# Second block's expert stage: routing's rest behind the second unit and its loads behind the first fetched rows; first block: rows split by VectorE instead of GpSimd

## The chip, the core and the metric

The kernel runs on one core of a Trainium2 chip. Its time is the device time of one execution in microseconds (us). Engines: TensorE (PE) multiplies matrices, VectorE (DVE) and ScalarE (ACT) work on tiles, GpSimd (POOL) does small things and issues indirect DMAs, SyncE (SP) issues the weight loads. Each engine runs its own instructions in a fixed order and waits on semaphores.

## What is computed

A transformer of 512 tokens by 1024 features, all in float32: a first block (mixer, cross attention, a mixture of experts), then a second block of two layers (token mixer, a mixture of experts). The change touches the three expert stages. Each picks for a token one of 4 groups and in it 2 of 8 experts; in the reference:

```
p_top, g_idx = lax.top_k(softmax(h @ w_rg + b_rg), 1)
e_top, e_local = lax.top_k(e_logits_of_group(g_idx), 2)
weights = p_top * softmax(e_top)
out[t] += weights * ((silu(x[t] @ w_gate[e]) * (x[t] @ w_up[e])) @ w_down[e])
```

An expert's hidden width is 512 in the first block (its three matrices are 2 MB each) and 256 in the second (1 MB each). In the second block, the token's row after the mixer is normalised, used by the experts, and also scaled by alpha, gain and bias for the residual sum.

## The kernel before

The expert stage (function moe, called by moe1 and moe2) works in units. A unit is up to 128 slots, shared by 2 or 3 experts (32 to 96 slots each); the second block has 14 units. Experts are ranked by how many tokens chose them, and the table of units says which rank gets how many slots. Experts 0 and 1 (second block) or 0 to 3 (first block) have fixed places, so their weights are loaded before routing is known; every other expert number is read by SP from a table (tab) that the routing computes.

Ahead of the stage, proj_cols multiplies by the output projection. After each of the four token tiles m, half(m, 1) makes the router's logits, the row factors (trs, with a power on GpSimd), chooses groups and experts (choose, a chain of small VectorE operations that ends in ohb), and writes the rows: in the second block to DRAM (zd), in the first by split_rows into a high part and a low part (xhi, xlo), which PE later multiplies with one-hot matrices.

route() then ranks experts and gives each token its slots. In the second block begin() turns the slots of unit 0 into token numbers and issues the indirect DMA that fetches its 128 rows (load_rows, tile xg, 0.5 MB). The rest of the routing is the function rest(): gate weights with two exponentials on ScalarE, slots of the overflow, a transpose on PE (L1156), two broadcasts on PE (L1164) into rows 2 and 3 of R["rows"], from which slot_weights makes the factor ws of each unit, and the expert table of the overflow.

The loop over units (L1552 and on) does for unit u: load gate and up weights and run unit_up (PE L1266, then hid, the transposes hT of L1272), fetch(u + 3), turn_rows of unit u + 1 (PE L1384, ScalarE L1386), and unit_down of unit u - 1 (yp L1291, yh and yl scaled by ws, then comb L1300/L1301, added to x). Order matters in two ways: the program order and priorities decide each engine's instruction order, and SP's queue is served in order, so a load that waits holds all loads behind it. Tiles for weights come from 5 + 6 buffers; a load waits until PE has freed its buffer.

In unit 0 of the second block a piece is put behind the last fetch's instruction (got["last"]): rest() and, for each tile, rows(m), two VectorE operations over 1024 columns that make the residual rows (L1684, L1685). In the first block rest() stands in the same place without rows(m).

Of the kernel before, what the change touches and what calls it, by code (L numbers as in the profile page):

```python
# [8 lines left out]
F32 = mybir.dt.float32  # L9
# [4 lines left out]
AF = mybir.ActivationFunctionType  # L14
OP = mybir.AluOpType
# [59 lines left out]
class Net:  # L75
# [910 lines left out]
    def split_rows(self, z, scale, m, hi, lo):  # L986

        h3, l3 = [t[m // 2][:, m % 2 * 1024:m % 2 * 1024 + 1024].rearrange("t (k p) -> t k p", k=8) for t in (hi, lo)]
        n = 1024 if scale is None else 512
        for a in range(0, 1024, n):  # L990
            src, p = z[:, a:a + n], slice(a // 8, (a + n) // 8)
            if scale is not None:
                t = self.k2("zs")
                self.nc.scalar.activation(t, src, AF.Copy, scale=scale)
                src = t
            src = src.rearrange("t (p k) -> t k p", k=8)
            self.nc.scalar.activation(h3[:, :, p], src, AF.Copy)
            last = self.nc.gpsimd.tensor_tensor(l3[:, :, p], src, h3[:, :, p].bitcast(F32), op=OP.subtract)
        return last

    def chooser(self):

# [237 lines left out]
    def load(self, W, e, k0, ahead, t=None, cols=slice(None)):  # L1240

        k, n = W.shape[1] // 128, W.shape[2]
        kn = 2048 // n
        if t is None:
            t = self.wtile(kn, n, ahead)
        src = W[e:e + 1] if isinstance(e, int) else W[bass.ds(e, 1)]
        self.nc.sync.dma_start(t[:, :, cols], src.rearrange("o (p k) n -> p (o k) n", k=k)[:, k0:k0 + kn, cols])
        return t

    def unit_up(self, xe, at, cols, wt, F, picking=None):  # L1250
# [138 lines left out]
    def moe(self, x, y, Wo, measure, norm, router, Wg, Wu, Wd, F, block, alpha=None, rows=None, prep=None, finish=None):  # L1389
# [11 lines left out]
        dram = block == 2  # L1401
        if dram:
            zd = self.keep.tile([512, 1024], F32, name="zd", tag="zd", bufs=2)
# [6 lines left out]
        else:  # L1410
            hi, lo = [[self.b8(n, F32R) for _ in range(2)] for n in ("xhi", "xlo")]
        lps = self.paux("lps")
        L, choose, choice = self.chooser()
        stats, split = {}, {}
        copy = nc.vector.tensor_copy if ws is None else (lambda o, i: nc.scalar.activation(o, i, AF.Copy))

        self.loaded, self.early = {}, {}

        def loads():
            for k0 in range(0, 8, 2048 // F):  # L1420
                for key, W in (("g", Wg), ("u", Wu)):
                    for e in (0, 1):
                        self.early[key, e, k0] = self.load(W, e, k0, True)
# [18 lines left out]
        def half(m, c):  # L1442
            with self.tc.high_priority():
                self.logits(x[m], m, c, wr, lps, copy)
                stats[m] = measure(m, c)
            if c:
                shift, rs = stats[m]
                off = rb
                with self.tc.high_priority():
                    if shift is not None:  # L1450
                        off = L[:, m, 4:40]
                        nc.vector.scalar_tensor_tensor(off, ws, shift, rb, op0=OP.mult, op1=OP.add)
                    for i in (m, 4 + m):
                        nc.vector.scalar_tensor_tensor(L[:, m, 4:40], lps[:, i * 36:i * 36 + 36], rs, off, op0=OP.mult, op1=OP.add)
                        off = L[:, m, 4:40]
                    choose(m)
                    if static == 4:
                        static_slots(m)
                left = norm(m, *stats[m])
                if dram:  # L1460
                    nc.scalar.dma_start(zd[m * 128:(m + 1) * 128, :], x[m])
                else:
                    split[m] = self.split_rows(x[m], left, m, hi, lo)

        self.proj_cols(y, Wo, self.add_to(x, alpha), lambda m: half(m, 0), lambda m: half(m, 1), loads)
        for e in (0, 1) if block == 1 else (0,):
# [8 lines left out]
        got = {}  # L1475
# [15 lines left out]
            with self.tc.high_priority():  # L1491
                one_hot(S0, 256, got[0], range(3, 4))
        def begin(S2):
            got["first"], _ = self.load_rows(zd, self.first_tokens(S2))

        R, rest = self.route(L, choice, self.tables[block], begin if dram else None)
        S2 = R["S2"]
# [14 lines left out]
        def expert(at):  # L1512
            return nc.values_load(R["tab"][0:1, at], engines=[mybir.EngineType.SP], min_val=0, max_val=31)
# [5 lines left out]
        def own_rows(at):  # L1519
            if dram:  # L1520
                return DTs.pop(at if isinstance(at, float) else "more"), self.slot_weights(R["rows"], at)
            return self.slot_rows(R, at)

        def before_down(es, at, ahead=True):
            return self.unit_weights("d", Wd, es, ahead), *own_rows(at)

        def down(hT, cols, es, at, ahead=True, finish=None, pre=None):
            wt, DT, ws = pre or before_down(es, at, ahead)
            self.unit_down(hT, cols, wt, F, DT, ws, x, finish)
# [14 lines left out]
        def fetch(u):  # L1544
            if u < len(units):
                DTs[128.0 * u], rowsof[u], _, got["last"] = self.fetch(zd, R["rows"], 128.0 * u)
# [17 lines left out]
        for u, unit in enumerate(units):  # L1564
            es = [(r, r if r < static else expert(slice(r, r + 1))) for r, _ in unit]
            cols, a0 = [], 0
            step = 32 if len({w for _, w in unit}) > 1 else unit[0][1]
            for i, (_, w) in enumerate(unit):
                cols += [(a0 + a, step, i) for a in range(0, w, step)]
                a0 += w  # L1570
            last = u == len(units) - 1
            if last:
                pre = before_down(*late[0][2:])
                down(*late.pop(), pre=pre)
                after = own_rows(128.0 * u)
            now = up(*((xe[u // 2][:, u % 2], 0) if dram else (xe[u // 2], u % 2 * 128)), cols, es), cols, es, 128.0 * u
            if last:
                pre = self.unit_weights("d", Wd, es, True, 2), *after
            if u == 0:
                if dram:  # L1580
                    with self.tc.issue_after(got["last"].ins):
                        rest()
                        for m in range(4):
                            rows(m)
                else:
                    with self.tc.issue_after(got["last"].ins):
                        rest()
            if u == 8 and prep is not None:
                prep()
            if dram:  # L1590
                fetch(u + 3)
                turn(u + 1)
            elif u % 2 and u + 1 < len(units):
                xe[u // 2 + 1] = pick(u + 1)
            while len(late) > (u in LAG[block]):
                down(*late.pop(0))
            late.append(now)
# [4 lines left out]
        n = nc.values_load(R["tab"][0:1, 64:65], min_val=0, max_val=32)  # L1602
        with self.tc.For_i(0, n) as iv:
            es, cols = [("further", expert(bass.ds(iv + 32, 1)))], [(0, 128, 0)]
# [683 lines left out]
```

## Time and profile before

| | us |
|---|---|
| median of 3 runs (2622.02 to 2631.01) | 2626.03 |
| profiled execution | 2632.68 |
| its span | 2630.8 |
| PE busy (92% of the span) | 2419.8 |
| VectorE busy (53%) | 1400.1 |
| ScalarE busy (35%) | 925.2 |
| GpSimd busy (10%) | 272.0 |

The stages follow one another: the first block's expert stage lies between about 430 and 1000 us of the span, those of the second block between about 1490 and 1800 and between 2300 and 2610. All times of rows are microseconds from the span's start. A wait is idle time of an engine, put down to what ended it. The clock column is the granted TensorE clock as a share of full speed: 1.00 is 2.4 GHz, 0.50 is 1.2 GHz.

### The profile page before, as it was taken

How to read it: one execution, taken by the hardware profiler on the slowest of the kernel's cores; microseconds unless marked ns; L12 is line 12 of the kernel's file. 1: busy time of each engine (PE TensorE's matmuls, PEld its weight loads, DVE VectorE, ACT ScalarE, POOL GpSimd, SP SyncE). 2: the span in 40 equal slices, each digit the busy share in tenths (PEclk: the TensorE clock that was granted, in tenths of full speed). 3: DMA queues.
4: the chain of work that ended last, by engine and by line, in shares of the span. 5: the costliest groups of instructions: out<-in, count | busy, mean ns of one | idle time of the engine just before them, and what ended most of it. 6: DMA issues, size and time to landing. Idle time of an engine off the chain costs nothing. (4 is left out here: it accounts for less than half of the span.)

```text
span 2630.8 us, 37791 instructions
## 1 busy us (share of the span) xinstructions
PE 2419.8 (92%) x14261; PEld 1579.4 (60%) x14261; DVE 1400.1 (53%) x3094; ACT 925.2 (35%) x1825; POOL 272.0 (10%) x444
## 2 busy tenths in 40 slices
PE   7898998899889998999999789998899999969995
PEld 6787887533334346677788644545577778735552
DVE  5568535432223236865645555446865644665455
ACT  6545533201111013655444132224554543322222
POOL 1143021000010001000020100104100010000001
PEclk9999999999999988999999889999999999979998
DMA  5214322779999976122223479994312223378993
GB/s 179 80 65 142 118 80 98 298 316 403 408 404 406 406 297 183 40 57 72 65 96 122 176 310 374 413 408 122 102 49 64 72 89 120 136 283 345 419 419 142
DMA packets 153047, 551.20 MB, mean 210 GB/s; under 512 B 20539, under 2 KB 48473, under 8 KB 105243
## 3 DMA queue, kind: packets, MB, share of 16 engines
q1 hardware_dynamic: 144458, 523.68, 52.1%
q0 software_dynamic: 6960, 20.33, 2.2%
q10 hardware_dynamic: 1440, 4.72, 0.5%
q8 instruction: 114, 1.87, 0.3%
q14 instruction: 75, 0.61, 0.1%
HBM read 538.19 MB, written 10.49 MB: 209 GB/s over the span
## 5 line engine op out<-in xcount | busy, mean ns | idle before, releaser
L248 DVE TENSOR_TENSOR wlo<-raw,whi 128x512 fp32r<-128x512 f32 (+2 forms) x368 | 258.4, 707 | 306.5 <-ACT whi L247 269.7
L247 ACT ACTIVATE whi<-raw 128x512 fp32r<-128x512 f32 (+2 forms) x368 | 215.8, 590 | 418.7 <-PE pacc L268 299.6
L267 PE MATMUL pacc<-hbh,whi 128*128 128x512 f32 (+1 forms) x768 | 309.2, 403 | 0.2 <-ACT whi L247 0.2
L269 PE MATMUL pacc<-hbh,wlo 128*128 128x512 f32 (+1 forms) x768 | 304.7, 397 | 1.1 <-DVE wlo L248 1.1
L268 PE MATMUL pacc<-hbl,whi 128*128 128x512 f32 (+1 forms) x768 | 304.0, 396 | 0.0
L1266 PE MATMUL gp<-we,xe 128*32 128x256 f32 (+3 forms) x2264 | 262.6, 433 | 5.7 <-DMA we<-in_w_gate_dram 5.0
L1303 DVE TENSOR_TENSOR x<-comb,x 128x512 f32<-128x512 f32 x304 | 191.7, 685 | 36.3 <-PE comb L1301 34.4
L1266 PE MATMUL gp<-wx,xe 128*32 128x256 f32 (+3 forms) x1608 | 201.9, 420 | 0.0
L1266 PEld LDWEIGHTS gp<-we,xe 128*32 128x32 f32 (+1 forms) x2264 | 113.2, 118 | 119.8 <-issue 62.8
L1268 ACT ACTIVATE hid<-gp 128x256 f32<-128x256 f32 (+1 forms) x41 | 18.5, 452 | 445.1 <-PE gp L1266 445.1
L1291 PE MATMUL yp<-we,hidT 128*32 128x512 f32 (+1 forms) x824 | 173.1, 605 | 1.1 <-ACT hidT L1274 0.7
L267 PEld LDWEIGHTS pacc<-hbh,whi 128*128 128x128 f32 (+1 forms) x768 | 144.3, 188 | 41.8 <-issue 8.5
L269 PEld LDWEIGHTS pacc<-hbh,wlo 128*128 128x128 f32 (+1 forms) x768 | 144.4, 188 | 36.1 <-issue 2.9
L268 PEld LDWEIGHTS pacc<-hbl,whi 128*128 128x128 f32 (+1 forms) x768 | 144.7, 188 | 31.3 <-issue 2.0
L1300 PE MATMUL comb<-yh,DT 128*128 128x512 f32 x328 | 135.8, 436 | 6.5 <-ACT yh L1293 6.2
L1294 DVE SCALAR_TENSOR_TENSOR yl<-yp,ws,yh 128x512 fp32r<-128x512 f32 x82 | 60.5, 749 | 144.3 <-ACT yh L1293 131.7
L1269 DVE TENSOR_TENSOR hid<-up,hid 128x512 f32<-128x512 f32 x13 | 9.0, 692 | 218.5 <-PE up L1266 218.5
L1291 PE MATMUL yp<-wx,hidT 128*32 128x512 f32 (+1 forms) x568 | 123.3, 602 | 1.6 <-ACT hidT L1274 1.0
L1301 PE MATMUL comb<-yl,DT 128*128 128x512 f32 x328 | 122.4, 400 | 1.9 <-DVE yl L1294 1.9
L1266 PEld LDWEIGHTS gp<-wx,xe 128*32 128x32 f32 (+1 forms) x1608 | 83.8, 113 | 55.8 <-issue 32.6
L1300 PEld LDWEIGHTS comb<-yh,DT 128*128 128x128 f32 x328 | 60.4, 188 | 86.9 <-ACT yh L1293 39.2
L1266 PE MATMUL up<-we,xe 128*32 128x512 f32 (+1 forms) x336 | 93.5, 645 | 13.5 <-DMA we<-in_w_up_dram 13.5
(704 smaller groups left out, 4693.2 us busy)
## 6 DMA issues: line engine op xcount, KB each, us to landing
raw<-in_w_in_dram SPq DMA_DIRECT2D x44, 1024.0 KB, 5.0
we<-in_w_down_dram SPq DMA_DIRECT2D x43, 1024.0 KB
we<-in_w_gate_dram SPq DMA_DIRECT2D x39, 1024.0 KB
we<-in_w_exp_up_dram SPq DMA_DIRECT2D x34, 1024.0 KB, 21.0
wx<-in_w_exp_gate_dram SPq DMA_DIRECT2D x34, 1024.0 KB, 20.9
we<-in_w_up_dram SPq DMA_DIRECT2D x33, 1024.0 KB, 4.9
wx<-in_w_exp_down_dram SPq DMA_DIRECT2D x32, 1024.0 KB, 10.2
wx<-in_w_up_dram SPq DMA_DIRECT2D x31, 1024.0 KB, 11.7
```

Source lines behind the costliest of these rows:

```text
L247: nc.scalar.activation(hi[:, :ncols], src, AF.Copy)
L248: nc.vector.tensor_tensor(lo[:, :ncols], src, hi[:, :ncols].bitcast(F32), op=OP.subtract)
L267: nc.tensor.matmul(o, hi[:, a], h.hi(k)[:, :ntok], start=k == 0, stop=False)
L268: nc.tensor.matmul(o, hi[:, a], h.lo(k)[:, :ntok], start=False, stop=False)
L269: nc.tensor.matmul(o, lo[:, a], h.hi(k)[:, :ntok], start=False, stop=k == kt - 1)
L1266: nc.tensor.matmul(ps[s:s + w, :], xe[:, k, at + s:at + s + w], wt[key, i, k], start=k == 0, stop=k == 7)
L1268: nc.scalar.activation(h, gp, AF.Silu)
L1291: nc.tensor.matmul(yp[a:a + w, :], hT[:, k * 128 + a:k * 128 + a + w], d, start=k == 0, stop=k == nf - 1)
L1294: nc.vector.scalar_tensor_tensor(yl[c], yp, ws, yh[c].bitcast(F32), op0=OP.mult, op1=OP.subtract)
L1300: nc.tensor.matmul(ps, a, yh[c], start=True, stop=False)
L1301: nc.tensor.matmul(ps, a, yl[c], start=False, stop=True)
L1303: nc.vector.tensor_tensor(xs, ps, xs, op=OP.add)
```

## The change

Three edits.

1. split_rows (first block): ScalarE no longer writes the scaled row to a temporary tile; it writes the high part straight from x with the scale, and VectorE makes the low part as x * scale - high in one operation. GpSimd does nothing there any more.
2. load(): while self.behind is set, each weight load gets a dependency on that instruction. moe sets it in unit 1 of the second block to the DMA that fetched unit 0's rows.
3. In the second block, rest() is called after unit 1's unit_up instead of unit 0's, behind the fetch that unit 0 issued; rows(m) stays with unit 0.

```diff
--- before.py
+++ after.py
@@ -986,17 +986,10 @@
     def split_rows(self, z, scale, m, hi, lo):
 
         h3, l3 = [t[m // 2][:, m % 2 * 1024:m % 2 * 1024 + 1024].rearrange("t (k p) -> t k p", k=8) for t in (hi, lo)]
-        n = 1024 if scale is None else 512
-        for a in range(0, 1024, n):
-            src, p = z[:, a:a + n], slice(a // 8, (a + n) // 8)
-            if scale is not None:
-                t = self.k2("zs")
-                self.nc.scalar.activation(t, src, AF.Copy, scale=scale)
-                src = t
-            src = src.rearrange("t (p k) -> t k p", k=8)
-            self.nc.scalar.activation(h3[:, :, p], src, AF.Copy)
-            last = self.nc.gpsimd.tensor_tensor(l3[:, :, p], src, h3[:, :, p].bitcast(F32), op=OP.subtract)
-        return last
+        for a in range(0, 1024, 512):
+            src, p = z[:, a:a + 512].rearrange("t (p k) -> t k p", k=8), slice(a // 8, a // 8 + 64)
+            self.nc.scalar.activation(h3[:, :, p], src, AF.Copy, scale=scale)
+            self.nc.vector.scalar_tensor_tensor(l3[:, :, p], src, scale, h3[:, :, p].bitcast(F32), op0=OP.mult, op1=OP.subtract)
 
     def chooser(self):
 
@@ -1244,7 +1237,9 @@
         if t is None:
             t = self.wtile(kn, n, ahead)
         src = W[e:e + 1] if isinstance(e, int) else W[bass.ds(e, 1)]
-        self.nc.sync.dma_start(t[:, :, cols], src.rearrange("o (p k) n -> p (o k) n", k=k)[:, k0:k0 + kn, cols])
+        load = self.nc.sync.dma_start(t[:, :, cols], src.rearrange("o (p k) n -> p (o k) n", k=k)[:, k0:k0 + kn, cols])
+        if self.behind is not None:
+            self.tc.add_manual_dep(load.ins, self.behind.ins.name, mybir.DependencyInfo(mybir.DependencyClass.Sync, mybir.DependencyReason.DATA))
         return t
 
     def unit_up(self, xe, at, cols, wt, F, picking=None):
@@ -1411,10 +1406,11 @@
             hi, lo = [[self.b8(n, F32R) for _ in range(2)] for n in ("xhi", "xlo")]
         lps = self.paux("lps")
         L, choose, choice = self.chooser()
-        stats, split = {}, {}
+        stats = {}
         copy = nc.vector.tensor_copy if ws is None else (lambda o, i: nc.scalar.activation(o, i, AF.Copy))
 
         self.loaded, self.early = {}, {}
+        self.behind = None
 
         def loads():
             for k0 in range(0, 8, 2048 // F):
@@ -1460,7 +1456,7 @@
                 if dram:
                     nc.scalar.dma_start(zd[m * 128:(m + 1) * 128, :], x[m])
                 else:
-                    split[m] = self.split_rows(x[m], left, m, hi, lo)
+                    self.split_rows(x[m], left, m, hi, lo)
 
         self.proj_cols(y, Wo, self.add_to(x, alpha), lambda m: half(m, 0), lambda m: half(m, 1), loads)
         for e in (0, 1) if block == 1 else (0,):
@@ -1491,7 +1487,7 @@
             with self.tc.high_priority():
                 one_hot(S0, 256, got[0], range(3, 4))
         def begin(S2):
-            got["first"], _ = self.load_rows(zd, self.first_tokens(S2))
+            got["first"], got["fetched"] = self.load_rows(zd, self.first_tokens(S2))
 
         R, rest = self.route(L, choice, self.tables[block], begin if dram else None)
         S2 = R["S2"]
@@ -1568,6 +1564,7 @@
             for i, (_, w) in enumerate(unit):
                 cols += [(a0 + a, step, i) for a in range(0, w, step)]
                 a0 += w
+            self.behind = got["fetched"] if dram and u == 1 else None
             last = u == len(units) - 1
             if last:
                 pre = before_down(*late[0][2:])
@@ -1579,12 +1576,14 @@
             if u == 0:
                 if dram:
                     with self.tc.issue_after(got["last"].ins):
-                        rest()
                         for m in range(4):
                             rows(m)
                 else:
                     with self.tc.issue_after(got["last"].ins):
                         rest()
+            if u == 1 and dram:
+                with self.tc.issue_after(got["last"].ins):
+                    rest()
             if u == 8 and prep is not None:
                 prep()
             if dram:
```

The instruction orders at three places. First, SP at the start of the second block's stage, before (L1513 reads an expert number, ISA rows are address arithmetic, DMAHW and DMASW are the semaphores of hardware and software DMA queues):

```order
L1247 DMA wx<-in_w_exp_gate_dram 128x2048 [waits DMAHW2_49]
L1247 ISA
L1247 DMA wx<-in_w_exp_up_dram 128x2048 [waits DMAHW3_49]
L1513 TENSOR_LOAD tab
L1513 ISA x2
L1247 ISA
L1247 DMA wx<-in_w_exp_gate_dram 128x2048 [waits DMAHW4_49]
L1247 ISA
L1247 DMA wx<-in_w_exp_up_dram 128x2048 [waits DMAHW5_49,Pool_49]
L1247 ISA
L1247 DMA wx<-in_w_exp_down_dram 128x2048 [waits DMAHW6_49,Pool_49]
```


and with the change:

```order
L1240 DMA wx<-in_w_exp_gate_dram 128x2048 [waits DMAHW2_49]
L1240 ISA
L1240 DMA wx<-in_w_exp_up_dram 128x2048 [waits DMAHW3_49]
L1509 TENSOR_LOAD tab
L1509 ISA x2
L1509 TENSOR_LOAD tab
L1509 ISA x2
L1240 ISA
L1240 DMA wx<-in_w_exp_gate_dram 128x2048 [waits DMAHW4_49,DMASW3_49]
L1240 ISA
L1240 DMA wx<-in_w_exp_up_dram 128x2048 [waits DMAHW5_49,Pool_49]
L1240 ISA
L1240 DMA wx<-in_w_exp_down_dram 128x2048 [waits DMAHW6_49,Pool_49]
```


The first two loads (gate and up of expert 31, for unit 0) wait as before; the third, gate of expert 30 for unit 1, now also waits on DMASW3, the first fetch's semaphore. The two after it stand behind it, and the read for the next unit stands ahead.

Second, PE after the matmuls of unit 0 in the second block, before (hT is unit 0's hidden transpose, gat unit 1's rows):

```order
L1266 MATMUL gp<-wx,xe 32x256
L1272 MATMUL hT<-ident,hid 128x128 x2
L1156 MATMUL paux<-ident,route 8x128 x4
L1164 MATMUL paux<-trow,sel 128x512 x2
L1384 MATMUL gat<-ident,xg 128x128 x8
L1266 MATMUL gp<-we,xe 32x256 x3
```


and with the change, there and at the end of unit 1:

```order
L1267 MATMUL hT<-ident,hid 128x128 x2
L1379 MATMUL gat<-ident,xg 128x128 x8
...
L1286 MATMUL yp<-wm,hidT 32x512
L1267 MATMUL hT<-ident,hid 128x128 x2
L1149 MATMUL paux<-ident,route 8x128 x4
L1286 MATMUL yp<-wm,hidT 32x512 x2
L1286 MATMUL yp<-wx,hidT 32x512
L1286 MATMUL yp<-wm,hidT 32x512 x3
L1286 MATMUL yp<-wx,hidT 32x512
L1157 MATMUL paux<-trow,sel 128x512 x2
L1379 MATMUL gat<-ident,xg 128x128 x8
```


The routing's two groups (L1156 and L1164 before, L1149 and L1157 now) moved from between unit 0's hT and unit 1's rows to behind unit 1's hT, with unit 0's yp matmuls between them, and nine yp matmuls stand ahead of that hT where there were five.

Third, VectorE in the first block, the choosing chain of the first token tile, before:

```order
L1454 SCALAR_TENSOR_TENSOR route<-lps,trs,route 128x36
L1013 MAX route<-route 128x8
L1014 MAX_INDEX route<-route 128x8
...
L1021 CAST route<-route 128x2
L1022 TENSOR_SCALAR route<-iota,route 128x32
L1024 TENSOR_SCALAR route<-iota,route 128x32
L1023 SCALAR_TENSOR_TENSOR ohb<-iota,route 128x32
```


and with the change:

```order
L1450 SCALAR_TENSOR_TENSOR route<-lps,trs,route 128x36
L992 SCALAR_TENSOR_TENSOR xlo<-x_2476,trs,xhi 128x8x64
L1006 MAX route<-route 128x8
L992 SCALAR_TENSOR_TENSOR xlo<-x_2476,trs,xhi 128x8x64
L1007 MAX_INDEX route<-route 128x8
...
L1014 CAST route<-route 128x2
L1015 TENSOR_SCALAR route<-iota,route 128x32
L1017 TENSOR_SCALAR route<-iota,route 128x32
L1016 SCALAR_TENSOR_TENSOR ohb<-iota,route 128x32
L850 TENSOR_TENSOR x_2477<-pacc,x_2477 128x512
```


The two low parts stand inside the chain, ahead of the index search, and the next tile's addition (L850) comes directly after ohb, ahead of the slot arithmetic of L1435 and on (now L1431). On PE the small matmul that waits for ohb (tri) stands five projection matmuls later for the first two tiles.

## Rows read from the trace of the kernel before

**Rows 1.** Page, part 2: busy tenths of PE and of the DMA engines, 40 slices.

```profile
PE   7898998899889998999999789998899999969995
...
DMA  5214322779999976122223479994312223378993
```

**Rows 2.** Waits of PE, 1490 to 1530: total us, times, longest us.

```profile
PE gat L1384 <- DMA xg<-zd,tki: 8.0, 1, 8.0
PE paux L1156 <- DVE route L1153: 3.9, 1, 3.9
```

**Rows 3.** Waits of PE, 2300 to 2340, the second layer.

```profile
PE gat L1384 <- DMA xg<-zd,tki: 8.4, 1, 8.4
```

**Rows 4.** Timeline of SP, 1490 to 1530: start us, us, instruction.

```profile
1500.71 0.35 SPq L1247 DMA_DIRECT2D wx<-in_w_exp_gate_dram  x1
...
1502.37 0.33 SPq L1247 DMA_DIRECT2D wx<-in_w_exp_gate_dram  x1
```

**Rows 5.** Timeline of GpSimd (POOL), 1470 to 1545.

```profile
1505.01 1.05 POOL L1357 DMA_INDIRECT xg<-zd,tki  x1 [11.05 <-DVE tki L1375]
```

**Rows 6.** DMA queues, 1501 to 1505: packets, MB, share.

```profile
q1 hardware_dynamic: 145, 1.11, 78.5%
```

**Rows 7.** DMA queues and issues, 1505 to 1509; last figure us to landing.

```profile
q1 hardware_dynamic: 227, 1.68, 99.8%
...
xg<-zd,tki POOLq DMA_INDIRECT x1, 8.8
```

**Rows 8.** DMA issues, 1534 to 1536.

```profile
xg<-zd,tki POOLq DMA_INDIRECT x1, 4.3
```

**Rows 9.** Timeline of PE, from the first turned rows to the third; weight loads left out.

```profile
1513.94 1.30 PE L1384 MATMUL gat<-ident,xg 128*128 128x128 f32 x5 [8.01 <-DMA xg<-zd,tki]
...
1525.19 0.51 PE L1272 MATMUL hT<-ident,hid 128*128 128x128 f32 x2 [1.31 <-DVE hid L1269]
...
1529.55 1.02 PE L1156 MATMUL paux<-ident,route 128*8 128x128 f32 x4 [3.85 <-DVE route L1153]
...
1531.59 1.22 PE L1164 MATMUL paux<-trow,sel 8*128 8x512 f32 x2 [1.03 <-DVE trow L1158]
...
1532.74 1.55 PE L1384 MATMUL gat<-ident,xg 128*128 128x128 f32 x6
...
1545.16 0.51 PE L1272 MATMUL hT<-ident,hid 128*128 128x128 f32 x2
...
1545.51 1.05 PE L1384 MATMUL gat<-ident,xg 128*128 128x128 f32 x8
```

**Rows 10.** Windows: us, busy us (count) PE, PEld, DVE, ACT, POOL, clock, DMA share, GB/s.

```profile
1532.00:1536.00 4.00, 4.00 (x26) 2.33 (x29) 1.54 (x5) 3.19 (x9) 0.94 (x1) 0.50 0.06 18
1536.00:1540.00 4.00, 4.00 (x60) 2.06 (x56) 0.00 (x0) 0.80 (x3) 0.00 (x0) 0.71 0.39 127
```

**Rows 11.** Groups of VectorE (DVE), 1510 to 1534: count | busy us, mean ns | idle before.

```profile
L1684 DVE SCALAR_TENSOR_TENSOR x<-x,lngb 128x1024 f32<-128x1024 f32 x4 | 4.9, 1215 | 0.0
...
L1121 DVE TENSOR_REDUCE route<-route 128x4 f32<-128x16 f32 x1 | 0.2, 171 | 4.5 <-ACT route L1119 4.5
```

**Rows 12.** Waits of PE, 1530 to 1810, the stage's longest.

```profile
PE comb L1300 <- ACT yh L1293: 2.7, 5, 0.8
```

**Rows 13.** Groups of all engines, 420 to 475, first block.

```profile
L998 POOL TENSOR_TENSOR xlo<-zs,xhi 128x512 fp32r<-128x512 f32 x8 | 12.2, 1546 | 7.9 <-ACT xhi L997 7.9
...
L997 ACT ACTIVATE xhi<-zs 128x512 fp32r<-128x512 f32 x8 | 9.2, 1196 | 0.0
...
L1022 DVE TENSOR_SCALAR route<-iota,route 128x32 f32<-128x32 f32 x4 | 5.8, 1445 | 0.1
...
L1021 DVE CAST route<-route 128x2 f32<-128x2 uint32 x4 | 5.2, 1293 | 0.1
```

**Rows 14.** Groups of all engines, 1465 to 1500, second block.

```profile
L1022 DVE TENSOR_SCALAR route<-iota,route 128x32 f32<-128x32 f32 x4 | 1.0, 242 | 0.1
```

**Rows 15.** Page, part 5: a VectorE operation of this size, contiguous.

```profile
L1294 DVE SCALAR_TENSOR_TENSOR yl<-yp,ws,yh 128x512 fp32r<-128x512 f32 x82 | 60.5, 749 | 144.3 <-ACT yh L1293 131.7
```

**Rows 16.** Waits of PE, 420 to 520, first block.

```profile
PE paux L1434 <- DVE ohb L1023: 11.6, 4, 4.2
```


## The prediction

> **What bounds the kernel now.** I read the page first, then the stretches that the change touches, in order of time. On the page, TensorE (PE) has digits of 9 in most of the 40 slices, and the DMA engines are at 9 only in three runs of slices, late in the three expert stages [rows 1]. So an instruction on another engine is worth nothing by itself; what counts is idle time of PE, and whether the weight stream behind it can follow if PE starts sooner.
>
> In the second block's expert stage PE's waits have two large entries before the stage runs smoothly: 8.0 us for the first fetched rows (tile xg) and 3.9 us for the rest of the routing, line 1153 [rows 2]. The block's second layer has 8.4 us at the same place [rows 3]; I treat both layers as alike and work out the first.
>
> How the first wait comes about: SP issues the dynamic loads from 1500.71, those of the second unit from 1502.37 [rows 4]. GpSimd issues the row fetch at 1505.01 [rows 5]. Between 1501 and 1505 the weight queue moved 1.11 MB [rows 6]; between 1505 and 1509 it moved 1.68 MB and the fetch's queue has no line at all [rows 7]. This fetch took 8.8 us from issue to landing [rows 7], while one that was issued with no weight load in flight took 4.3 us [rows 8]. PE turns the first rows at 1513.94, and the first unit's matmuls end in the transposes at 1525.19 [rows 9]. Then PE stands until 1529.55 for the routing's transposes, runs two short groups of 1.02 and 1.22 us, and turns the second unit's rows at 1532.74 [rows 9]. During this the granted clock falls to 0.50, which is 1.2 GHz, and the matmuls of the second unit run their first part at it (0.50, then 0.71) [rows 10].
>
> **The change, part by part.** The profiled execution took 2632.7 us (span 2630.8), the median of the runs is 2626.0, 6.7 below; I work out a difference and subtract it from the median.
>
> *The loads of unit 1 wait for the first rows.* One wait is added on SP; behind it in SP's queue stand three loads (gate and up of expert 30, down of expert 31) and then the third unit's. Ahead of it stay two loads of 1.05 MB, 2.1 MB in all. 1.11 MB had gone by 1505 [rows 6], and 1.68 MB go in 4 us [rows 7], so the other 1.0 MB are through at 1507.4. The fetch then has the engines for itself. Its price lies between 4.3 us (empty queues [rows 8]) and 8.8 (no gain [rows 7]); since 2.4 of its first 4 us still meet weights I take 5.0, nearer to the empty case. That is **-3.8 us a layer** (0 to -4.5).
>
> Who waits for the wait: unit 1's matmuls need expert 30. Released at about 1510, its two loads and the one behind them are 3.1 MB, with two more row fetches of 0.5 MB each: 4.2 MB at 0.42 MB/us, 10 us, done near 1521. Unit 0 then ends near 1521 and unit 1's matmuls begin near 1523 (up part from 1526). So I cost this at nothing, with 2 to 6 us of cover; without it the end of the transfer would show one for one.
>
> *rest() goes behind unit 1.* PE's way from the transposes of unit 0 (1525.19) to the turn of unit 1 (1532.74) is 7.55 us; the same way one unit later, where no routing stands in it, is 0.35 (1545.16 to 1545.51) [rows 9]. So **-7.2 us**. The two short PE groups come back after unit 1: 1.02 and 1.22 us at the low clock, 1.1 at the high one; I take **+1.6** (1.1 to 2.2). With the hole gone the clock should stay at 1.0, 2.4 GHz: the turn and unit 1's matmuls ran at half speed from 1532.74 to about 1538.3 (a mean of 0.71 over 1536 to 1540 is 2.3 us at 0.5 [rows 10]), 5.6 us, worth 2.8; a short low spell may come one unit later, so **-2.0** (0 to -2.8).
>
> What covers rest() now: VectorE must finish it while PE does unit 1. VectorE first does the eight row operations of rows() (1.2 us each [rows 11]), which were mixed with it, then the next fetch's four instructions, then rest(). Its line 1121 waited 4.5 us on ScalarE's exponential [rows 11]; the exponentials now stand behind unit 1's evacuations, with unit 1's matmuls to hide them. The new order also puts nine yp matmuls ahead of unit 1's transposes, where before there were five, so PE has work if VectorE is 1 or 2 us late. I take **+1.0** (0 to +3). A layer: -3.8 -7.2 +1.6 -2.0 +1.0 = **-10.4**, two layers **-20.8**.
>
> What is late next: PE is then 10 us ahead of the old stage. Afterwards the loads wait for buffers that PE frees, so they move with it. In the old run no wait of PE in the stage was for a weight load; the largest of the stage is 2.7 us for ScalarE [rows 12]. So I let the gain through.
>
> *First block's split.* Removed: GpSimd's eight subtractions (L998, 12.2 us, 1.55 us each) and ScalarE's eight scalings. GpSimd and ScalarE are not the bound here; the effect is on VectorE's choosing chain: its two instructions L1021 and L1022 take 1.29 and 1.45 us while L998 runs [rows 13], and L1022 takes 0.24 in the second block, where GpSimd is idle [rows 14]. That is 1.2 us over for L1022 and at least 1.0 for the smaller L1021, so 2.2 us for each of four tiles. Added: eight operations on VectorE inside the same chain, each waiting for ScalarE's half (1.20 us, L997 [rows 13]). A plain one of this size takes 0.75 [rows 15]; GpSimd's strided one took 1.55; I take 1.2, since ScalarE's strided pass is 1.2 too. The second half's wait and one operation cost the chain 2.3 us. So the chain itself is even. PE's four waits for this chain are 11.6 us [rows 16]; the new order places the small matmul behind five more projection matmuls for tiles 0 and 1 and puts the next tile's addition ahead of the slot arithmetic, which lets the next tile start 1 to 2 us sooner, but the last tiles' chains are now mixed. I take **-1.5** (-3.5 to +3).
>
> Sum: -20.8 -1.5 = **-22.3**, so **2603.7, rounded 2604** (2610.4 for the profiled execution).
>
> **The rivals.** *Landing is not held up by the backlog* (2609). For it: the rows cannot tell how much of the fetch's first four microseconds is a wait behind weights and how much its own start. Then holding loads back gives only the fetch's own share of bandwidth, 0.52 MB at 0.42, 1.3 us instead of 3.8: 5 us less over both layers. Against it: 4 us without a packet of the fetch's queue [rows 7]. The Trainium skill (DMA: Bandwidth & Descriptors, Queues, rings and completion order) has each DMA engine take turns between the queues it has work for, packet by packet; by that a backlog in another queue costs the fetch no more than such a share, and this rival is what it would give. The trace agrees only in part: a stretch with none of the fetch's packets is not taking turns.
>
> *The rest of the routing becomes a wait one unit later* (2615). VectorE finishes late, PE stands before unit 1's routing transposes as it did before unit 0's (3.9 + 1.0 us, instead of my 1.0) and the clock falls again (no -2.0): +5.9 a layer, +11.8. For it: VectorE is in order and the rows() work and a fetch stand ahead. Against: 8 us of matmuls and the moved yp cover it.
>
> *Slower: the weight stream sets the end of the stage* (2640). The loads of unit 1 go out at 1510 instead of 1502.4, and all later ones stand behind them; the page shows the DMA engines full later in each stage [rows 1]. If the stage ended with its stream, each layer would lose these 7.6 us: +15.2 -1.5. It decides once less than 7.6 us of idle DMA time lie between the held loads and the full stretch. Against: the DMA share is 0.06 and 0.39 in eight microseconds after 1532 [rows 10], 6.2 us idle in these alone, and PE waits for no weight load there [rows 12].
>
> *The split costs the first block time* (2608). VectorE's strided operation takes GpSimd's 1.55 us and the last two chains mix badly: +3 instead of -1.5. Also possible that the scheduler's new order does less than the diff says; the order listing shows the wait on exactly the load of expert 30, so I give that no chance of its own.
>
> **How the numbers follow.** Forecast 0.60, landing 0.14, late routing 0.16, stream 0.04, first block 0.06. The range reaches from the better ends of the terms (about -4.4, -7.2, +1.1, -2.8, +0.5 a layer, -3.5 in the first block: -29, with 3 us for the runs' own spread: 2594) to the late-routing case with its spread (2617); the stream case and the tails stay out. 0.3% of this kernel is 7.9 us, about what a measurement can tell from no change. The forecast, the landing and first-block cases are all beyond it, and most of the late-routing case (-10.5): 0.88 faster; 0.08 within it, 0.04 slower.
>
> **What would show it.** Right: the first fetch lands about 5 us after issue, PE's wait for it falls from 8.0 to about 4; no wait on line 1153's successor between units 0 and 1; the way from unit 0's transposes to the turn of unit 1 is under 1 us; no low clock in unit 1; no wait of PE for expert 30. In the first block L1021's and L1022's successors take 0.2 us. Wrong: a landing still near 8.8 us, a new idle stretch of PE of 4 us or more behind unit 1, PE waiting for gate or up of expert 30, or expert stages no shorter although they began sooner.

## The result and the profile after

The changed kernel takes 2595.5 us (median of 4 runs, 2589.6 to 2603.6) against 2625.0 us: a ratio of 0.9887, 95% interval 0.9854 to 0.9919, so about 29.5 us less, between 21 and 38. A second set (e4_again, below) gives 0.9890 with a narrower interval, 0.9875 to 0.9905: 25 to 33 us. The forecast was 22 us less; the time lies inside the range, near its low end.

The lead at a few places in time, from the starts of the same instruction in both profiles (ScalarE's silu of a unit, GpSimd's first fetch of a layer):

| place | start before | start after | lead |
|---|---|---|---|
| first block, unit 0 | 494.6 | 490.8 | 3.8 |
| first block, unit 9 | 824.3 | 820.3 | 4.0 |
| first block, units 11 and 12 | 903.1, 969.2 | 897.0, 955.2 | 6.1, 13.9 |
| layer 1, first fetch | 1505.0 | 1491.1 | 13.9 |
| layer 1, units 0, 1, 2 | 1524.0, 1543.6, 1561.7 | 1506.3, 1515.9, 1535.9 | 17.7, 27.8, 25.7 |
| layer 1, units 5 and 13 | 1614.7, 1785.5 | 1590.1, 1760.6 | 24.6, 24.9 |
| layer 2, first fetch | 2314.3 | 2286.7 | 27.6 |
| layer 2, units 0, 1, 2 | 2333.3, 2353.0, 2371.0 | 2302.0, 2311.6, 2331.7 | 31.3, 41.3, 39.3 |
| layer 2, unit 13 | 2591.9 | 2553.4 | 38.5 |

Each layer gains 11 us (13.9 to 24.9; 27.6 to 38.5), the first block's start 3.8, of which 0.3 are there before the edited code begins. The 7.8 us between 903 and 969, the 2.1 before that and the 2.7 us between the layers lie where nothing was edited; the experiments come to them.

The second block first. PE's waits of the changed kernel, the stretch that answers to [rows 2] (total us, times, longest us):

```profile
PE gat L1379 <- DMA xg<-zd,tki: 4.0, 1, 4.0
```

The wait for the first rows went from 8.0 to 4.0 us, and the wait for the rest of the routing, 3.9 us before, has no line any more. In the second layer the 8.4 us of [rows 3] became:

```profile
PE gat L1379 <- DMA xg<-zd,tki: 4.6, 1, 4.6
```

The DMA queues after this fetch's issue at 1491.08, which answer to [rows 7]: first two rows of 1491 to 1493, then one of 1493 to 1495 (q1 carries the weights, q0 the fetched rows; packets, MB, share; the last figure of the issue's row is the time to landing):

```profile
q1 hardware_dynamic: 112, 0.84, 99.1%
...
xg<-zd,tki POOLq DMA_INDIRECT x1, 4.8
...
q0 software_dynamic: 133, 0.50, 68.6%
```

Half a megabyte of rows, nearly the whole fetch, moved between 2 and 4 us after the issue, and it landed after 4.8 us; in the kernel before not one of its packets had moved 4 us after the issue. When they began to move there, the fetch still shared the engines with the weights; these are its queues from 1509 to 1511:

```profile
q1 hardware_dynamic: 82, 0.55, 65.5%
q0 software_dynamic: 69, 0.28, 35.0%
```

PE's timeline, answering to [rows 9] (weight loads and other rows left out):

```profile
1495.96 1.94 PE L1379 MATMUL gat<-ident,xg 128*128 128x128 f32 x8 [3.97 <-DMA xg<-zd,tki]
...
1507.17 0.50 PE L1267 MATMUL hT<-ident,hid 128*128 128x128 f32 x2 [1.00 <-DVE hid L1264]
...
1507.51 1.06 PE L1379 MATMUL gat<-ident,xg 128*128 128x128 f32 x8
...
1518.27 0.50 PE L1267 MATMUL hT<-ident,hid 128*128 128x128 f32 x2
...
1518.61 0.60 PE L1149 MATMUL paux<-ident,route 128*8 128x128 f32 x4
...
1520.99 0.71 PE L1157 MATMUL paux<-trow,sel 8*128 8x512 f32 x2
...
1521.64 1.16 PE L1379 MATMUL gat<-ident,xg 128*128 128x128 f32 x8
```

From the transposes of unit 0 (hT, 1507.17) to the turn of unit 1 (1507.51) PE takes 0.34 us where it took 7.55. The routing's two groups (L1149, L1157) now stand behind unit 1's hT (1518.27), without a wait in front of them. The windows that hold unit 1's matmuls, for [rows 10] (columns as there):

```profile
1508.00:1512.00 4.00, 3.89 (x70) 2.39 (x72) 3.69 (x16) 3.91 (x10) 0.94 (x1) 1.00 1.02 421
1512.00:1516.00 4.00, 4.00 (x76) 2.28 (x72) 4.00 (x33) 2.08 (x5) 0.00 (x0) 1.00 1.01 426
```

The clock is 1.00, 2.4 GHz, where it was 0.50 and 0.71. PE's waits in the rest of the stage, for [rows 12]:

```profile
PE comb L1295 <- ACT yh L1288: 2.7, 6, 0.8
...
PE gp L1261 <- DMA we<-in_w_exp_up_dram: 0.8, 1, 0.8
```

One wait is new: 0.8 us for an up weight, at 1586, where the kernel before has none. The first block, groups of VectorE, for [rows 13] and [rows 14], and PE's waits there, for [rows 16]:

```profile
L992 DVE SCALAR_TENSOR_TENSOR xlo<-x,trs,xhi 128x512 fp32r<-128x512 f32 x8 | 9.8, 1225 | 0.9 <-ACT xhi L991 0.9
...
L1015 DVE TENSOR_SCALAR route<-iota,route 128x32 f32<-128x32 f32 x4 | 1.0, 240 | 0.1
...
L1014 DVE CAST route<-route 128x2 f32<-128x2 uint32 x4 | 0.7, 168 | 0.1
```

```profile
PE gat L1185 <- DVE D L1477: 3.7, 1, 3.7
PE paux L1430 <- DVE ohb L1016: 2.9, 2, 1.5
PE paux L979 <- DVE x L850: 2.1, 1, 2.1
```

L1014 and L1015, which were L1021 and L1022, take 0.17 and 0.24 us where they took 1.29 and 1.45. The added operation takes 1.23 us. PE's waits for ohb fell from 11.6 to 2.9 us, and two others came in their place, 3.7 us for the one-hot matrix D and 2.1 for the next tile's addition.

### The profile page after: what moved, and what is told of

Its sections match the earlier page's. It is cut to its first block, busy times and chain, and to the rows that moved or that the text cites. A ratio compares the mean times of both kernels' runs of the same rounds, so it can differ in the third digit from the quotient of the medians.

```text
span 2592.2 us, 37782 instructions
## 1 busy us (share of the span) xinstructions
PE 2401.4 (93%) x14261; PEld 1571.7 (61%) x14261; DVE 1399.4 (54%) x3102; ACT 920.7 (36%) x1817; POOL 261.5 (10%) x436
## 5 line engine op out<-in xcount | busy, mean ns | idle before, releaser
L1261 PE MATMUL up<-we,xe 128*32 128x512 f32 (+1 forms) x336 | 90.1, 618 | 13.3 <-DMA we<-in_w_up_dram 13.3
```

What stands on the lines that cost most here:

```text
L1261: nc.tensor.matmul(ps[s:s + w, :], xe[:, k, at + s:at + s + w], wt[key, i, k], start=k == 0, stop=k == 7)
```

## Experiments

All ratios are against the kernel before on the same chip. The first four give the parts.

**e1_split**: the kernel before with the new split_rows alone.

```
-                self.nc.scalar.activation(t, src, AF.Copy, scale=scale)
...
-            last = self.nc.gpsimd.tensor_tensor(l3[:, :, p], src, h3[:, :, p].bitcast(F32), op=OP.subtract)
+            self.nc.scalar.activation(h3[:, :, p], src, AF.Copy, scale=scale)
+            self.nc.vector.scalar_tensor_tensor(l3[:, :, p], src, scale, h3[:, :, p].bitcast(F32), op0=OP.mult, op1=OP.subtract)
```

> The split alone. By the changed kernel's trace the first block's unit 0 starts 3.8 us sooner and that lead holds to the unit at 824 us: 3.8 us off (ratio 0.9985), with the successors of L1021 and L1022 at 0.17 and 0.24 us and the second block as before (first fetch 8.8 us, gap 7.5 us before unit 1's turn). The prediction's own term was 1.5 off. Rival: the whole lead of 13.9 us that the changed kernel has at the end of that block belongs to the split (ratio 0.9947); then the stretch of low clock at 920 to 945 us of the kernel before must be absent here and return in e2 and e3.

Measured: 0.9971 (0.9959 to 0.9983), 7.6 us, at least 4.5 where 3.8 were expected. In its profile the lead grows from 0.6 at the first row factor (431.7) to 4.0 at unit 0, so 3.4 us belong to the edit, and it stays 3.6 to 4.1 until 903; then 7.9 us come on top before 969; e2, whose first block is unchanged, has them too, so they don't belong to the split. Layers: no gain in either (11.5 at layer 1's first fetch, 11.4 at its unit 13; 14.4 and 14.3 in layer 2), but 3.0 between them (see e0_before); 3.4 alone lies below the interval, 3.4 and these 3.0 are 6.4, which it holds.

**e2_hold**: the kernel before with the hold-back alone, the dependency in load included.

```
+            self.behind = got["fetched"] if dram and u == 1 else None
```

> The hold-back alone. Theory: first rows land about 4.8 us after issue instead of 8.8, unit 0 and everything behind it 3.8 us sooner in each layer, since the exponentials and so line 1121 move along: 7.6 us off (ratio 0.997). Rival: the rest of the routing, still in its old place, ends no sooner and takes the gain back as a longer wait in front of unit 1: 0 to 1 us off. Rival of the sharing only: landing near 7.5 us, 2.6 off.

Measured: 0.9964 (0.9952 to 0.9977), 9.4 us. Lead in layer 1 from 11.5 to 15.1, in layer 2 from 18.2 to 21.9: 3.6 and 3.7. PE's waits at the start of layer 1's stage:

```profile
PE gat L1386 <- DMA xg<-zd,tki: 4.2, 1, 4.2
PE paux L1156 <- DVE route L1153: 3.9, 1, 3.9
```

The first wait fell to 4.2 us while the second kept its 3.9: the rest of the routing moved along instead of taking the gain back, and the rival falls. So does the one of sharing only, at 2.6 us for both layers: the landing is 5.0 and 4.8 us, not 7.5.

**e3_rest**: the kernel before with rest() called in unit 1 alone.

```
-                        rest()
                         for m in range(4):
                             rows(m)
...
+            if u == 1 and dram:
+                with self.tc.issue_after(got["last"].ins):
+                    rest()
```

> The move of rest alone. Theory: additive, 7.0 us a layer as between units 0 and 5 of the changed kernel, 14 off (ratio 0.9947); first fetch still 8.8 us. Rival: without the hold the loads run early and the move's gain is the same but part of it is the clock, which stays low longer after the longer first wait: 10 off or less.

Measured: 0.9930 (0.9917 to 0.9944), 18.4 us, with the expected 14 just outside. Lead in layer 1 from 9.2 to 16.3, in layer 2 from 19.4 to 26.2: 7.1 and 6.8. The first rows are as late as ever:

```profile
PE gat L1384 <- DMA xg<-zd,tki: 8.2, 1, 8.2
```

Here too the step from unit 4 to unit 5 costs 1.0 us, with a wait of 0.7 us for an up weight, and in e2 it does not.

**e4_again**: the changed kernel unaltered. **e0_before**: the kernel before unaltered.

> The changed kernel once more, unaltered, for a second profile and more times. By the sum of the terms (3.8 + 10.7 + 10.9 = 25.4) a ratio of 0.9903; by the first comparison 0.9887. Theory: the stretch of low clock near 920 to 945 us that the kernel before showed and the first profile did not is chance and may be here.

> The kernel before, unaltered, for a second profile of it. Theory: its first profile held two stretches of low clock that were chance (8 us near 930, 3 us near 1800 to 1870); here they are absent, the end of the first block's experts is 8 us sooner and the execution lies near 2622. Rival: they belong to the kernel before and are there again (near 2632, or shown in the same places).

Measured: e4 0.9890 (0.9875 to 0.9905), its layers 11.0 and 12.6 us shorter than the first profile of before (1.4 of the 12.6 lie between units 8 and 9, where the change's first profile has a short spell of low clock, 0.86 over 2448 to 2460, and e4 has 1.00); e0 0.9991 (0.9981 to 1.0001). The profile of e0 has the same stretch of low clock as the first one; its windows, with the columns of [rows 10]:

```profile
924.00:928.00 4.00, 4.00 (x15) 2.76 (x14) 0.00 (x0) 0.37 (x1) 0.00 (x0) 0.50 1.01 420
...
932.00:936.00 4.00, 4.00 (x15) 2.27 (x15) 0.00 (x0) 0.37 (x1) 0.00 (x0) 0.50 0.06 23
```

The same stretch of time in e2, whose first block is the code of before:

```profile
924.00:928.00 4.00, 4.00 (x25) 2.48 (x26) 0.00 (x0) 0.73 (x2) 0.00 (x0) 1.00 1.01 422
...
932.00:936.00 4.00, 4.00 (x14) 1.86 (x12) 2.65 (x6) 0.69 (x1) 0.00 (x0) 1.00 0.94 391
```

and a window of e6 (below), whose first block is the code of the change:

```profile
924.00:928.00 4.00, 4.00 (x13) 2.27 (x12) 0.00 (x0) 0.66 (x2) 0.00 (x0) 0.50 1.00 418
```

PE is busy without a pause in all three, at 0.50 in e0 and e6 and at 1.00 in e2. The stretch costs 8 us, and it comes with either form of the first block and stays away with either: both profiles of before and that of e6 have it, those of the change, of e4 and of all other experiments do not. So it is no part of the change's worth, and e0's expectation that it would be absent was wrong, though the rival that ties it to the code of before falls with e6. Both profiled executions of the old code, 2632.7 and 2632.5 us, lie 7 and 10 us above the medians of their runs (2626.0 and 2622.4), which fits these 8 us. The 2.7 to 3.1 us that e1, e2, e3 and the change win between the layers are of the same kind. They come in two steps of 1.6 us, where the first profile of before has two short spells of low clock; first its rows, then the change's for the same work:

```profile
1864.00:1872.00 8.00, 7.40 (x22) 5.13 (x23) 6.19 (x11) 6.33 (x9) 0.00 (x0) 0.79 0.05 5
1894.00:1902.00 8.00, 6.32 (x23) 4.17 (x24) 6.42 (x19) 2.46 (x11) 0.00 (x0) 0.79 0.01 2
...
1839.00:1847.00 8.00, 6.91 (x26) 4.81 (x26) 6.62 (x14) 7.89 (x14) 0.00 (x0) 1.00 0.12 19
1867.00:1875.00 8.00, 6.78 (x31) 4.48 (x30) 6.29 (x20) 3.95 (x14) 0.00 (x0) 1.00 0.01 3
```

The second profile of before has the first spell earlier (0.79 over 1808 to 1816, then 1.00 over 1864 to 1872). The 1.6 us that the change won between 824 and 870 have the same cause: a short spell in the first profile of before (0.79 over 832 to 840) that its own lacks (1.00 over 826 to 838). Short spells come and go between profiles of one code, and no edit is near these. How often they stand in the timed runs is not shown.

**e5_pool_back**: what had been taken from GpSimd, given back without use.

```
+            t = self.k2("zs").rearrange("t (k p) -> t k p", k=8)
+            self.nc.gpsimd.tensor_tensor(t, src, h3[:, :, p].bitcast(F32), op=OP.subtract)
```

> The changed kernel, with the eight subtractions put back on GpSimd into a tile that nobody reads (the output is the same; no engine's order changes but GpSimd's). Theory (GpSimd's operation and VectorE's get in each other's way): L992 or the small operations behind it stretch by 1.5 to 3 us a tile, PE's waits in the choosing stage grow, and the first block gives back 4 to 9 us against the changed kernel (ratio to before 0.9905 to 0.993). Rival (the gain came from the new order alone, the next tile's addition ahead of the slot arithmetic): no instruction of VectorE gets longer, 0.989 as without it.

Measured: 0.9922 (0.9906 to 0.9938); unit 0's silu starts 9.9 us later than in the change, though the stage's first row factor came 0.6 sooner: 10.5 us, a little more than the 4 to 9 expected. VectorE's rows for the first tile, then GpSimd's:

```profile
432.72 2.76 DVE L992 SCALAR_TENSOR_TENSOR xlo<-x,trs,xhi 128x512 fp32r<-128x512 f32 x1 [0.37 <-ACT xhi L991]
...
435.45 2.27 DVE L992 SCALAR_TENSOR_TENSOR xlo<-x,trs,xhi 128x512 fp32r<-128x512 f32 x1
```

```profile
432.76 4.10 POOL L994 TENSOR_TENSOR zs<-x,xhi 128x512 f32<-128x512 f32 x2 [1.42 <-ACT xhi L991]
```

The low part takes 2.76 and 2.27 us instead of 1.25, and GpSimd's two operations 4.10 us instead of 3.05 in the kernel before: they wait for each other. By the times it is 8 us (0.9922 against 0.9890). So the gain of the split hangs on GpSimd being still, and the rival (order alone) falls. PE pays in both waits:

```profile
PE gat L1187 <- DVE D L1479: 7.0, 1, 7.0
PE paux L1432 <- DVE ohb L1018: 6.6, 2, 4.0
```

**e6_hold_third** and **e7_hold_fourth**: how long may the loads be held?

```
-                DTs[128.0 * u], rowsof[u], _, got["last"] = self.fetch(zd, R["rows"], 128.0 * u)
+                DTs[128.0 * u], rowsof[u], got["load", u], got["last"] = self.fetch(zd, R["rows"], 128.0 * u)
...
-            self.behind = got["fetched"] if dram and u == 1 else None
+            self.behind = got["load", 2] if dram and u == 1 else None
```

(That is e6; e7 has got["load", 3].)

> The changed kernel, with unit 1's loads held behind the third unit's rows instead of the first's. Landing of the three fetches: about 4.8, 4.5 and 5 us; the loads go out near 1502 instead of 1496, gate of expert 30 lands near 1505 and up near 1508, unit 1 begins at 1508.7: theory, no wait of PE or up to 1 us, ratio 0.989 as the changed kernel. Rival (the weight stream sets the end of the stage): the 6 us show in each layer, 0.9935.

> As before it, but held behind the fourth unit's rows, whose fetch is issued at 1511 and lands near 1515: past the cover. PE waits for gate of expert 30 from 1508.7 to about 1518.5, 10 us, with the clock low after it (+2): 12 us a layer, 24 in all, ratio 0.998. Rival (the hold's length matters little, loads catch up later through the spare DMA time): PE loses under 5 us a layer.

Measured: e6 0.9892 (0.9874 to 0.9910), e7 0.9986 (0.9975 to 0.9997). In e6 the load of gate 30 goes out 12.1 us after the first fetch's issue, in the change 4.8: 7.3 us later, and between the first fetch and unit 13 neither layer loses more than 0.3 us (up to 1.0 us is missing at unit 5 and won back). In e7 it goes out 24.5 us after that issue, and PE waits:

```profile
PE gp L1261 <- DMA wx<-in_w_exp_gate_dram: 9.1, 1, 9.1
```

A layer is 13 us longer (the lead against the change falls by 13.1 and 13.3 us between first fetch and unit 13). So the cover of the hold is about 10 us (19.7 us later, 9.1 of them waited for). A layer loses more than the 9.1 us: PE comes out of the wait at a granted clock of 0.50 (1520 to 1524) and 0.54 (1524 to 1528), which is part of it. Of the 13.6 to 14 us lost at unit 1 less than 1 us is won back by unit 13.

**e8_split_later**: the low parts behind the choice instead of within it.

```
-            V.tensor_scalar(oh2[:, m], iota, f[:, 2:3], None, op0=OP.is_equal)
+            self.chosen = V.tensor_scalar(oh2[:, m], iota, f[:, 2:3], None, op0=OP.is_equal)
...
+            with self.tc.issue_after(self.chosen.ins):
+                self.nc.vector.scalar_tensor_tensor(l3[:, :, p], src, scale, h3[:, :, p].bitcast(F32), op0=OP.mult, op1=OP.subtract)
```

> The changed kernel, with VectorE's two low parts of each tile put behind the choice of that tile (behind ohb) instead of into its chain. In the changed kernel the chain from the row factor to ohb is 5.6 us, of which 2.4 are the two low parts; without them PE's waits for ohb (2.9 us for two tiles) go, but the next tile's addition stands behind the low parts. Theory (the chain sets the pace): first block 2 to 3 us sooner, ratio 0.988. Rival (VectorE's total work sets the pace, the order does not matter): within 1 us of the changed kernel.

Measured: 0.9877 (0.9856 to 0.9897), median 2590.0. The first tile's chain from the logits to ohb is 3.0 us instead of 5.6. The profile's lead over the change is 1.3 us at the stage's first row factor and 5.6 at unit 1, so 4.3 us for the edit, more than the 2 to 3 expected, and it is kept to the end. PE's waits in that stage:

```profile
PE gat L1186 <- DVE route L1009: 3.0, 1, 3.0
...
PE paux L979 <- DVE x L850: 1.7, 3, 0.9
```

There is no line for ohb any more (2.9 us in the change). The time alone does not tell it from the change; the trace does.

**e9_hold_all** and **e10_hold_up**: unit 0's loads held too, both of them or the second.

```
-            self.behind = got["fetched"] if dram and u == 1 else None
+            self.behind = got["fetched"] if dram and u < 2 else None
```

(That is e9; in e10 the dependency is set in unit 0 only between its gate and its up load.)

> The changed kernel, with unit 0's two loads (gate and up of expert 31) held behind the first rows too. Landing of the fetch 4.3 to 4.5 us instead of 4.8 to 5.3, 0.5 us won; but gate of expert 31 goes out only then and is 1.05 MB behind two row fetches. Theory: PE waits 3 us or more for it at the start of unit 0, with the clock still low: 2 to 5 us a layer slower than the changed kernel, ratio 0.991 to 0.993. Rival: the loads come in time, ratio 0.9885.

> The changed kernel, with only the up load of unit 0 held too (gate goes out as before). At the fetch's issue 1 MB less is queued: landing 4.3 to 4.5 us instead of 4.8 to 5.3; up of expert 31 lands about 1500 where PE needs it near 1502. Theory: 0.5 us a layer won, not resolved by the time, seen in the landing and in PE's wait for the first rows (3.5 us or less for 4.0), no wait for the up weights. Rival: the landing does not depend on what is queued any more (4.8), or PE waits for up of expert 31.

Measured: e9 0.9918 (0.9901 to 0.9934); e10 0.9880 (0.9862 to 0.9899), median 2591.8. In e9:

```profile
PE gat L1379 <- DMA xg<-zd,tki: 3.6, 1, 3.6
...
PE gp L1261 <- DMA wx<-in_w_exp_gate_dram: 2.8, 1, 2.8
```

The rows come 0.4 us sooner, and the gate weights 2.8 us late; a layer loses 3.5 and 3.8 us by unit 0. In e10 the queues of the first 2 us after the issue, and PE's wait:

```profile
q0 software_dynamic: 9, 0.04, 11.2%
q1 hardware_dynamic: 10, 0.02, 2.2%
...
xg<-zd,tki POOLq DMA_INDIRECT x1, 4.3
```

```profile
PE gat L1379 <- DMA xg<-zd,tki: 3.5, 1, 3.5
```

With next to no weights on the way only 9 of the fetch's packets move in the first 2 us, and the landing still takes 4.3 us. PE's first wait is 0.5 us shorter, of which 0.2 a layer are left by unit 0; this is too little for the times to tell.

**e11_both**: e8 and e10 together.

> The low parts behind the choice (as in e8_split_later) and unit 0's up load held (as in e10_hold_up) together, as the version that may beat both kernels. From the profiles of these two: 4.2 us in the first block and 0.3 us a layer against the changed kernel, 5 in all: near 2589, ratio to before 0.987. Theory: the two add up. Rival: the up load's hold helps only because of its place against the other loads, and with the block before it shifted it gives nothing: 0.988, as the first of them alone.

Measured: 0.9881 (0.9864 to 0.9899), median 2590.1. Its profile goes from 0.6 us behind the change at the stage's first row factor to 3.7 ahead at unit 1, the same 4.3 as in e8, but is only 0.9 ahead at unit 12 of the first block: 1.0 us goes between units 3 and 4 and 1.7 between 820 and 864, where no edit is near. In both stretches it has a short spell of low clock (0.86 over 572 to 584, 0.57 over 828 to 832) that e8 and the change lack. That the two add up is not shown. e8 and e11 have the lowest medians of all, some 3 to 5 us below the change, which the intervals do not tell apart.

## Why the prediction was right, and where its sizes were off

**The hold-back (-3.8 a layer): right.** The landing was put at 5.0 us and measured 4.8 and 5.3; unit 0's lead grew by 3.8 and 3.7, and e2 alone gives 3.6 and 3.7. The rival of sharing only (1.3 a layer) falls. Of its 4.0 us the rows give about half to each cause: the first packets came after 2 us instead of 4, and then they had the engines almost alone (0.50 MB in 2 us) instead of sharing them (0.28 MB in 2 us). The Trainium skill (DMA: Bandwidth & Descriptors, Queues, rings and completion order), with its turns between queues packet by packet, agrees with that second half (0.55 MB of weights moved beside the 0.28). Why the first packets come later behind a longer backlog, no run shows.

**Its cover (nothing, with 2 to 6 us to spare): right, and wider than put.** e6 holds 7.3 us longer for nothing, e7 puts the cover at about 10. The rival that the stream sets the end falls: 7.3 us later cost nothing, and only a hold 19.7 us longer cost 13.

**rest() behind unit 1 (-7.2): measured -7.2**, 7.55 to 0.34 us. **The clock (-2.0): -2.9**, what is left of the 10.1 by which unit 1's lead grew; the low clock does not come back one unit later, so the step that allowed for such a spell was the one too careful. **The moved groups (+1.6): +2.1** between units 1 and 2. **VectorE late (+1.0): 0.** Its last operation before the transposes (L1146) ended at 1516.9, PE's came at 1518.6: 1.7 us to spare, and the late-routing rival falls. **Not foreseen: +1.1** at unit 5 of layer 1, where the sentence "I let the gain through" stood. PE, 10 us ahead, waits 0.8 us for an up weight there (e3 has it without any hold, e2 does not), so it goes with being early; that this is its cause is not shown. With 0.3 at unit 11: 3.8 + 7.2 + 2.9 - 2.1 - 1.1 + 0.3 = 11.0 in layer 1, against 10.4; layer 2 has 10.9.

**The first block (-1.5, between -3.5 and +3): -3.5**, at the end of its bounds. "The chain itself is even" held for three of the four tiles: 5.5 us from the router's logits to ohb before and 5.6 after in the first. The third, which is mixed with the next tile's addition and the one-hot matrix D, went from 5.4 to 7.7, as "the last tiles' chains are now mixed" had it. The mis-sized term is what the new order lets the next tile win, put at 1 to 2 us: the row factors of the next three tiles come 2.4, 2.1 and 1.5 us sooner, each upon the last, 5.9 us in all, and 2.4 of them are lost again by unit 0, where the new wait of 3.7 us for D stands. e1 gives 3.4 for it alone, and e5 shows its cause; the rival of a first block that gets longer falls.

**The sum.** Traced terms: 3.5 + 11.0 + 10.9 = 25.4 us, inside the intervals of both sets (21 to 38, 25 to 33). The three parts timed alone add up to 35 us, each with 3 or 4 us of uncertainty; each of their profiles leads by about 3 us between the layers for want of two short spells of low clock. If their timed runs do the same, the 35 counts these 3 us three times; that is argued, not shown.

## What to carry to other kernels

Where an engine stands for a small transfer, look at what was queued just ahead of it: a wait on a big load that has 10 us of slack bought 4 us of a small one, and the slack can be measured by holding longer until PE waits. Work that is needed one unit later should be issued one unit later, and the price of the hole that goes is the idle time plus the low clock behind it. Before leaving work on a third engine, see whether it slows the second: two operations of 1.3 and 1.45 us were 0.17 and 0.24 without it.

## What the runs showed of the hardware

- PE fully busy for 16 us at a granted clock of 0.50, in some executions of either kernel and not in others, on the same matmuls: 8 us. One profile of each kernel therefore misleads by more than a term of the sum; here two profiles of before agreed to about 1 us throughout, and both held it. The short spells moved a lead by another 1.6 us each. Ahead of the long one PE did the same whether that came or not: it was busy for 7.2 of the 10 us from 900 in the first profile of before, and for 7.2 of the same 10 us of work in e6, which has the spell, and in e1, e2 and the change, which have not. Nothing in these runs shows what decides it.
- VectorE and GpSimd stopped each other for whole operations. In the kernel before, L1021 and L1022 each ended 0.02 to 0.05 us after the GpSimd operation beside it, in all four tiles (in the first tile at 436.44 after 436.41, and at 437.92 after 437.87); in e5 it was the low part. The Trainium skill (SBUF — State Buffer, Who interferes with whom) has it so: the two engines share one pair of ports, which one instruction holds until it ends; casts and tensor_scalar operations can run in modes that take the pair, and an operation with two SBUF inputs contends with a GpSimd operation that reads SBUF. The traces agree for all three kinds: the cast L1021, the tensor_scalar L1022, and in e5 L992.
- A fetch's first packets moved 1.8 us after its issue with almost no weights ahead (e10), 2.3 us with 1.0 MB (the change: two loads of 1.05 MB issued, 1.11 MB moved), and 4.2 us with 4.1 MB (before: five loads issued, 1.11 MB moved).
